# Two transformer blocks on one core: float32r masks, second score products over 128 rows, and ten modulation chunks on VectorE

## The chip, the cores and the metric

The kernel runs on one core of a Trainium2 chip. Its five engines work side by side, each through its own list of instructions in order: TensorE (PE in the profile; its weight loads are shown as PEld), VectorE (DVE), ScalarE (ACT), GpSimd (POOL) and SyncE (SP), which here only issues DMAs. The metric is the device time of one execution in microseconds (us), as the median of several runs. Everything before the launch (splitting and reordering of the weights into the layout that the kernel loads) is outside of it.

## The reference

Two transformer blocks over 512 tokens of width 1024, one after the other, in float32.

```python
def first_block(x, c, ...):
    mod = silu(c) @ ada_w + ada_b
    sh1, sc1, ga1, sh2, sc2, ga2 = split(mod, 6)
    h = rmsnorm(x, pre_mix_g) * (1.0 + sc1) + sh1
    y = hybrid_mixer(h, ...)          # gated conv branch + stick-breaking attention
    x = x + ga1 * rmsnorm(y, post_mix_g)
    h = rmsnorm(x, pre_ffn_g) * (1.0 + sc2) + sh2
    y = swiglu_ffn(h, ...)
    return x + ga2 * rmsnorm(y, post_ffn_g)

def second_block(x, positions, ...):
    h = rms_norm(x, attn_norm_w)
    y_ret = retention_group(...)      # 8 heads of 64, scores with decay, causal
    y_mla = mla_group(...)            # 8 latent heads, softmax, causal
    x = x + concat(y_ret, y_mla) @ w_out
    x = x + conv_ffn(rms_norm(x, ffn_norm_w), ...)
    return rms_norm(x, final_norm_w)
```

In stick-breaking attention a query row t sees the keys s < t (strictly), with a = sigmoid(z) times the product of sigmoid(-z) of the keys between; in the latent attention it sees s <= t with a softmax. Both are computed for 128 queries at a time against the keys up to them.

## The kernel before

**Splitting.** Each float32 operand of a large product is split into a hi part (a float32r cast, on ScalarE) and a lo part (the rest, `lo_of`, L210, on VectorE or GpSimd). `mm3` (L205 to L207) adds three float32r products: hi x hi, lo x hi and hi x lo. A product has a stationary operand of up to 128 rows and 128 columns and a moving operand of 128 rows and up to 512 columns.

**Weights.** They come in slabs of 128x1024 in the order of `ORDER`. `emit_slab` issues the load from SP into `w_st` (two buffers, tag "st" of the pool `ring`), casts it to `w_hi` on ScalarE (L187) and makes `w_lo` (L210); the hi and lo tiles are four deep each. A slab is 24 products of 512 columns (8 blocks of rows times 3).

**Order.** The program is written in the order of its stages; the framework lays it out on the engines by its own simulated timeline, so instructions of neighbouring steps interleave. Pools open and close as stages pass, and a tile in a new pool waits for the tiles that had its place in SBUF.

**Modulation chunks.** `ada_acc` (L367 ff.) multiplies a chunk of 256 columns of ada_w by silu(c). Two loads `ad` of 512 KB hold the eight blocks of 128 rows; eight products with 32 stationary columns each (L373, two records each, so 16 in the trace), four side by side in the columns of the array, leave a partial sum in four quarters of a PSUM tile, which VectorE copies (L378). A product with ones then sums over partitions: `ada_cols` (L384) makes a shift and scale for 128 columns of h, `ga_row` (L404 to L406) a row of 256 gate values over all partitions. Eight chunks feed the first norm, eight the second (six of them between stick heads, two beside the merge), four rows of `grow1` are made beside the merge (loop over p after the heads: output projection of the attention, gating, `mh`), and four rows of `grow2` in the first feed-forward, at m = 4, 8, 12 and 16 of its 22 steps (`fin_extra`). Beside the merge the chunks are loaded into the pool `mtmp`, in the feed-forward into the ring's "st" tiles.

**Stick heads.** `evac_stat` makes of q, for each of two heads of a pair (b = 0, 1), a stationary tile with hi in one half of the rows and lo in the other; `evac_mov` makes of k a moving tile with hi in both halves, and `ml`, where each half holds the lo of one head. A block of scores is then a product over 128 rows (L685: hi x hi and lo x hi), one over 64 rows (L686: hi x lo) and the mask (L687), a bf16 product of the identity with a tile of 0 and -1e30, 128 columns. There are 8 heads of 4 blocks, with 128, 256, 384 and 512 columns. The pipeline has three steps per head (scores, transposes, product with v), with slabs of q, k and gate between them, and the depthwise conv's taps run on VectorE, ScalarE and GpSimd beside them.

**Retention.** `ret_head` does the same with roles exchanged (L1057, L1058), without a mask product: GpSimd zeroes the upper triangle (L1067). **Latent heads.** `mla_head` uses `mm3` for a block and then the causal mask (L1195) as a bf16 product.

Small tiles that the change touches: `part` (L672, a spare tile in `combine`), `adab1` (L153, ada_b + 1), `cs4` (L946, four copies of cos and sin, filled at L985 and transposed at L1128), `ident` (128 columns of the constants, used by all transposes, L231).

## Time and profile before

| | |
|---|---|
| median of 3 runs | 1425.65 us (1425.45 to 1426.05) |
| the profiled execution's own time | 1426.3 us |
| its span, first to last instruction | 1424.6 us |
| TensorE busy | 1378.3 us, 97% |
| VectorE busy | 731.9 us, 51% |
| ScalarE busy | 582.1 us, 41% |
| GpSimd busy | 325.1 us, 23% |
| mean granted TensorE clock | 0.991 |

A row of a timeline gives start, duration, engine, line, operation, out<-in, the part of the array that a product uses (rows*columns), shape and type, count, and in brackets the idle time ahead of it and what ended it. Successive products overlap, since each is shown until its last result lands: a 512-column product is shown with 0.39 us, but the next one starts after 0.23. For the cost of a product the distance between two starts is read, not the duration.

### The profile page before, as it was taken

The page shows a single profiled execution, that of the slowest core. Times are in us where ns is not written, and L with a number is a line of the kernel's source. Part 1 is how long each engine was busy: PE and PEld are TensorE (multiplying, and loading weights), DVE is VectorE, ACT ScalarE, POOL GpSimd, SP SyncE. Part 2 cuts the span into 40 slices and gives each one's busy share as a digit, 9 for nine tenths or more (in the row PEclk, how much of TensorE's full clock was granted, in tenths as well). Part 3 has the DMA queues.
Part 4 walks back from the last instruction along what each step waited for, and adds up shares of the span by engine and source line. Part 5 has one row for each costly group of instructions (what it writes and reads, how often), then busy time and mean ns, then how long its engine had stood idle before and what let it go on. Part 6 is the DMA issues. An engine that isn't in the chain of part 4 may idle for free. (4 is left out here: it accounts for less than half of the span.)

```text
span 1424.6 us, 17617 instructions
## 1 busy us (share of the span) xinstructions
PE 1378.3 (97%) x6846; PEld 1119.7 (79%) x6846; DVE 731.9 (51%) x1132; ACT 582.1 (41%) x953; POOL 325.1 (23%) x329
## 2 busy tenths in 40 slices
PE   6999999999989999999999899999999999999998
PEld 4786777877878888888887788787888888888886
DVE  3299868254365332232333754688256655554334
ACT  4457655322244222222223525668345333333222
POOL 2189745321150000000002533377220000000000
PEclk9998999999999999999999999999999999999999
DMA  9422133564323344333232322001233323232321
GB/s 332 139 83 81 58 103 108 170 201 146 133 68 118 126 126 132 112 104 104 89 104 79 126 95 89 30 16 60 83 110 104 101 92 104 89 104 89 104 90 73
DMA packets 44324, 152.20 MB, mean 107 GB/s; under 512 B 4881, under 2 KB 7057, under 8 KB 44241
## 3 DMA queue, kind: packets, MB, share of 16 engines
q1 hardware_dynamic: 42720, 145.90, 31.0%
q0 software_dynamic: 1376, 4.97, 0.9%
q8 instruction: 54, 0.88, 0.3%
q14 instruction: 30, 0.24, 0.1%
q10 hardware_dynamic: 144, 0.21, 0.0%
HBM read 146.86 MB, written 4.19 MB: 106 GB/s over the span
## 5 line engine op out<-in xcount | busy, mean ns | idle before, releaser
L187 ACT CAST w_hi<-w_st 128x1024 fp32r<-128x1024 f32 (+2 forms) x217 | 225.3, 1039 | 395.6 <-PE ps_p L206 125.9
L210 DVE TENSOR_TENSOR w_lo<-w_st,w_hi 128x1024 fp32r<-128x1024 f32 (+2 forms) x179 | 222.4, 1244 | 258.5 <-ACT w_hi L187 256.6
L205 PE MATMUL ps_p<-hh,w_hi 128*128 128x512 f32 (+1 forms) x740 | 278.0, 382 | 1.9 <-ACT hh L266 1.2
L206 PE MATMUL ps_p<-hl,w_hi 128*128 128x512 f32 (+1 forms) x740 | 279.1, 378 | 0.4 <-POOL hl L210 0.4
L207 PE MATMUL ps_p<-hh,w_lo 128*128 128x512 f32 (+1 forms) x740 | 277.9, 376 | 1.4 <-DVE w_lo L210 1.4
L242 POOL TENSOR_TENSOR r<-q,mhalf 128x1 f32<-128x1 f32 x36 | 21.4, 595 | 768.4 <-DVE q L238 723.9
L205 PEld LDWEIGHTS ps_p<-hh,w_hi 128*128 128x128 f32 x740 | 139.4, 190 | 30.8 <-ACT hh L266 2.5
L207 PEld LDWEIGHTS ps_p<-hh,w_lo 128*128 128x128 f32 x740 | 140.4, 190 | 27.7 <-DVE w_lo L210 2.5
L206 PEld LDWEIGHTS ps_p<-hl,w_hi 128*128 128x128 f32 x740 | 140.6, 190 | 26.0 <-POOL hl L210 1.6
L205 PE MATMUL ps_c<-hh,w_hi 128*128 128x512 f32 (+1 forms) x354 | 130.4, 368 | 3.1 <-ACT hh L266 2.0
L206 PE MATMUL ps_c<-hl,w_hi 128*128 128x512 f32 (+1 forms) x354 | 130.0, 368 | 1.1 <-POOL hl L210 1.1
L207 PE MATMUL ps_c<-hh,w_lo 128*128 128x512 f32 (+1 forms) x354 | 128.6, 363 | 0.0
L210 POOL TENSOR_TENSOR w_lo<-w_st,w_hi 128x1024 fp32r<-128x1024 f32 (+1 forms) x38 | 93.1, 2455 | 67.0 <-ACT w_hi L187 47.1
L210 DVE TENSOR_TENSOR gl<-gf,gh 128x512 fp32r<-128x512 f32 x44 | 30.4, 690 | 105.6 <-ACT gh L869 105.5
L869 ACT CAST gh<-gf 128x512 fp32r<-128x512 f32 x44 | 27.4, 622 | 135.1 <-PE ps_p L206 124.1
L205 PEld LDWEIGHTS ps_c<-hh,w_hi 128*128 128x128 f32 x354 | 67.3, 190 | 15.9 <-ACT hh L266 2.5
L206 PEld LDWEIGHTS ps_c<-hl,w_hi 128*128 128x128 f32 x354 | 66.9, 189 | 11.7 <-POOL hl L210 1.3
L207 PEld LDWEIGHTS ps_c<-hh,w_lo 128*128 128x128 f32 x354 | 67.1, 189 | 11.0 <-issue 0.8
L207 PE MATMUL ps_p<-w_hi,gl 128*128 128x512 f32 x176 | 68.5, 389 | 0.0
L206 PE MATMUL ps_p<-w_lo,gh 128*128 128x512 f32 x176 | 68.5, 389 | 0.0
L205 PE MATMUL ps_p<-w_hi,gh 128*128 128x512 f32 x176 | 68.5, 389 | 0.0
L510 DVE SCALAR_TENSOR_TENSOR ps_c<-upad,vec,ps_c 128x512 f32<-128x512 f32 x87 | 60.6, 747 | 0.7
(423 smaller groups left out, 2536.0 us busy)
## 6 DMA issues: line engine op xcount, KB each, us to landing
ad<-in_ada SPq DMA_DIRECT2D x48, 512.0 KB, 4.0
w_st<-in_w_fin SPq DMA_DIRECT2D x44, 512.0 KB, 3.7
w_st<-in_w_up SPq DMA_DIRECT2D x44, 512.0 KB, 3.7
w_st<-in_w_win SPq DMA_DIRECT2D x22, 512.0 KB, 3.7
w_st<-in_w_fout SPq DMA_DIRECT2D x22, 512.0 KB, 3.6
w_st<-in_w_down SPq DMA_DIRECT2D x22, 512.0 KB, 3.7
w_st<-in_w_gate SPq DMA_DIRECT2D x16, 512.0 KB, 3.7
w_st<-in_w_wo SPq DMA_DIRECT2D x16, 512.0 KB, 3.7
```

What stands on the lines that cost most here:

```text
L187: nc.scalar.copy(w_hi[:, :n], w_st[:, :n])
L205: nc.tensor.matmul(out=out, lhsT=lh, rhs=rh, start=start, stop=False)
L206: nc.tensor.matmul(out=out, lhsT=lh, rhs=rl, start=False, stop=False)
L207: nc.tensor.matmul(out=out, lhsT=ll, rhs=rh, start=False, stop=stop)
L210: (eng or nc.vector).tensor_tensor(out=out, in0=src, in1=hi.bitcast(F32), op=ALU.subtract)
L242: nc.gpsimd.tensor_tensor(out=r, in0=q, in1=mhalf[:, 0:1], op=ALU.pow)
L510: nc.vector.scalar_tensor_tensor(out=out, in0=src, scalar=w, in1=acc, op0=ALU.mult, op1=ALU.add)
L869: nc.scalar.copy(gh, gf[:, k, :])
```

## The change

Masks: the three bf16 tiles go. The identity is loaded by itself (`eye`) and cast to a float32r tile `identr`, which also serves the transposes. `mask_tile` loads one 128x128 mask by SP ahead of the stick heads, and one ahead of the latent heads, and casts it on VectorE; the mask product is float32r. Second score products: `ml` becomes a list of two tiles, one for each head of a pair, with zeros in the other half of the rows (`zero_padded`, eight GpSimd copies in all, two sets of two tiles for the stick heads and two for retention), and the product runs over all 128 rows. Modulation: from the merge on `ADA.vector` is set, and `ada_acc` makes the chunk by one scaling and seven multiply-adds of 128x256 on VectorE. Beside this, `part`, `adab1` and the bf16 mask tiles go, `cs4` moves into the latent pool (and its copies with it), and a few tiles take other places (`early_gate`, `split_o`). What was cut from the diff are renamed tags and the smaller constants.

```diff
+        if ADA.vector:
+            acc = ap_.tile([128, 256], F32, tag="acc", name="acc", bufs=ADA.nacc)
+            for hf, ad in enumerate(ads):
+                for b in range(4):
+                    cc = cact[:, 4 * hf + b, 0:1]
+                    if hf == 0 and b == 0:
+                        nc.vector.tensor_scalar(out=acc, in0=ad[:, b, :], scalar1=cc, scalar2=None, op0=ALU.mult)
+                    else:
+                        nc.vector.scalar_tensor_tensor(
+                            out=acc, in0=ad[:, b, :], scalar=cc, in1=acc, op0=ALU.mult, op1=ALU.add
+                        )
+            return acc, pt()[:, 256:512]
...
-    masks = adp.tile([128, 256], F32, tag="masks", name="masks", bufs=1)
-    nc.gpsimd.dma_start(out=masks, in_=a["masks"])
+    eye = adp.tile([128, 128], F32, tag="eye", name="eye", bufs=1)
+    nc.gpsimd.dma_start(out=eye, in_=a["eye"])
     nc.gpsimd.dma_start(out=pos, in_=a["positions"])
+    nc.vector.tensor_copy(identr, eye)
...
-    nc.vector.tensor_scalar(out=adab1, in0=vec[:, _o:_o + 48], scalar1=1.0, scalar2=None, op0=ALU.add)
-    nc.vector.tensor_copy(identb, ident)
-    nc.vector.tensor_copy(strictb, masks[:, 0:128])
-    nc.vector.tensor_copy(causalb, masks[:, 128:256])
+    for _i in (_o + 8, _o + 32):
+        nc.vector.tensor_scalar(
+            out=vec[:, _i:_i + 8], in0=vec[:, _i:_i + 8], scalar1=1.0, scalar2=None, op0=ALU.add
+        )
...
+    def mask_tile(p, j):
+
+        m = p.tile([128, 128], F32R, tag="mask", name="mask", bufs=1)
+        raw = p.tile([128, 128], F32, tag="sp0", name="raw")
+        nc.sync.dma_start(out=raw, in_=a["masks"][:, 128 * j:128 * j + 128])
+        nc.vector.tensor_copy(m, raw)
+        return m
...
+    def zero_padded(p, name):
+
+        t = [[p.tile([128, S], F32R, tag=f"{name}{i}{b}", name=f"{name}{i}{b}", bufs=1) for b in range(2)] for i in range(2)]
+        for i in range(2):
+            for b in range(2):
+                o = halves_of(b)[1]
+                nc.gpsimd.tensor_copy(t[i][b][o], zero[o].broadcast_to([64, S]))
+        return t
+
+    def evac_mov(ps, p, ml):
         t = []
-        ml = p.tile([128, S], F32R, tag="ml", name="ml")
         for b in range(2):
             mt = p.tile([128, S], F32R, tag=f"mv{b}", name=f"mv{b}")
             o, z = halves_of(b)
             nc.scalar.copy(mt[o], ps[o])
             nc.scalar.copy(mt[z], ps[o])
-            lo_of(ml[o], ps[o], mt[o])
+            lo_of(ml[b][o], ps[o], mt[o])
...
-    def combine(ps, h, dst, p):
+    def combine(ps, h, dst):
         o, z = halves_of(h % 2)
-        part = p.tile([128, S], F32, tag="part", name="part", bufs=1)
-        nc.scalar.copy(part[o], ps[z])
-        nc.vector.tensor_tensor(out=dst[o], in0=ps[o], in1=part[o], op=ALU.add)
+        nc.scalar.copy(dst[o], ps[z])
+        nc.vector.tensor_tensor(out=dst[o], in0=ps[o], in1=dst[o], op=ALU.add)
...
-            nc.tensor.matmul(out=z[:, :n], lhsT=qs[b][o, qb], rhs=kl[o, :n], start=False, stop=False)
-            nc.tensor.matmul(out=z[:, qb], lhsT=identb, rhs=strictb, start=False, stop=True)
+            nc.tensor.matmul(out=z[:, :n], lhsT=qs[b][:, qb], rhs=kl[b][:, :n], start=False, stop=False)
+            nc.tensor.matmul(out=z[:, qb], lhsT=identr, rhs=strict, start=False, stop=True)
...
-            qk[p] += evac_mov(ps, qkp)
+            qk[p] += evac_mov(ps, qkp, kz[p % 2])
...
+    strict = mask_tile(apool, 0)
+    kz = zero_padded(qkp, "kz")
...
-    ADA.pool, ADA.tag, ADA.bufs = mtmp, "ad", 2
+    ADA.pool, ADA.tag, ADA.bufs, ADA.vector = mtmp, "ad", 2, True
...
+    rstk, qz = {}, zero_padded(rt, "qz")
...
+        rstk[p] = (ks,) + evac_mov(ps, rt, qz[p % 2])
...
-            nc.tensor.matmul(out=z[:, :n], lhsT=ks[b][o, js], rhs=ql[o, kb * 128:], start=False, stop=True)
+            nc.tensor.matmul(out=z[:, :n], lhsT=ks[b][:, js], rhs=ql[b][:, kb * 128:], start=False, stop=True)
...
+        cs4 = mla.tile([128, NT, 4, 32], F32)
+        for j in range(4):
+            nc.gpsimd.tensor_copy(cs4[:, :, j, :], sinp if j % 2 else cosp)
...
-            nc.tensor.matmul(out=z[:, qb], lhsT=identb, rhs=causalb, start=False, stop=True)
+            nc.tensor.matmul(out=z[:, qb], lhsT=identr, rhs=latent["causal"], start=False, stop=True)
...
-    latent["mt"] = mt
+    latent.update(mt=mt, causal=mask_tile(mt, 1))
```

## Rows read from the trace of the kernel before

**Rows 1.** Rows of the page, section 1 (busy time, share of the span and instructions of each engine) and of section 6 (DMA issues: out<-in, engine, operation, count, KB each, median us to landing).

```profile
PE 1378.3 (97%) x6846; PEld 1119.7 (79%) x6846; DVE 731.9 (51%) x1132; ACT 582.1 (41%) x953; POOL 325.1 (23%) x329
...
ad<-in_ada SPq DMA_DIRECT2D x48, 512.0 KB, 4.0
```

**Rows 2.** Rows of TensorE's waits (tile and line that waited, what ended it, us in total, times, longest).

```profile
PE ps_t L373 <- DMA ad<-in_ada: 11.9, 1, 11.9
...
PE ps_p L685 <- ACT mv L616: 2.1, 1, 2.1
```

**Rows 3.** Rows of TensorE's timeline in a plain stretch between stick heads; from the first row to the last there are nineteen products of 512 columns, one start after another.

```profile
150.64 0.39 PE L206 MATMUL ps_p<-hl,w_hi 128*128 128x512 f32 x1
...
154.97 0.39 PE L207 MATMUL ps_p<-hh,w_lo 128*128 128x512 f32 x1
```

**Rows 4.** Rows of TensorE's timeline around a chunk in the first feed-forward.

```profile
592.50 0.39 PE L207 MATMUL ps_p<-hh,w_lo 128*128 128x512 f32 x1
...
592.82 1.07 PE L373 MATMUL ps_t<-ad,cact 128*32 128x256 f32 x16
...
594.16 0.40 PE L206 MATMUL ps_p<-hl,w_hi 128*128 128x512 f32 x1
```

**Rows 5.** Rows of TensorE's timeline around a chunk beside the merge; the four products of 512 columns are the one of the first row, two in the middle (lines left out) and one ahead of the last row.

```profile
300.69 0.40 PE L207 MATMUL ps_p<-oh,w_lo 128*128 128x512 f32 x1
...
301.02 0.64 PE L373 MATMUL ps_t<-ad,cact 128*32 128x256 f32 x8
...
303.18 0.39 PE L205 MATMUL ps_c<-hh,w_hi 128*128 128x512 f32 x1
```

**Rows 6.** Rows of VectorE's groups by line in 290 to 342 us (line, engine, operation, out<-in, shapes, count, busy us, mean ns of one, idle before).

```profile
L378 DVE COPY acc<-ps_t 128x256 f32<-128x256 f32 x6 | 2.5, 421 | 2.8 <-PE ps_t L373 2.7
...
L406 DVE SCALAR_TENSOR_TENSOR grow<-grow,gr 128x256 f32<-128x256 f32 x3 | 1.3, 418 | 0.0
```

**Rows 7.** Rows of TensorE's timeline around an isolated block of a stick head.

```profile
237.09 0.39 PE L685 MATMUL ps_c<-mv,st 128*128 128x512 f32 x1
...
237.41 0.49 PE L686 MATMUL ps_c<-ml,st 64*128 64x512 f32 x1
...
237.83 0.23 PE L687 MATMUL ps_c<-strictb,identb 128*128 128x128 bf16 x1
...
238.18 0.40 PE L207 MATMUL ps_p<-hh,w_lo 128*128 128x512 f32 x1
```

**Rows 8.** Rows of TensorE's timeline at the end of a stick head's product with v (L650), successive rows.

```profile
177.25 0.28 PE L650 MATMUL ps_t<-ah,v 128*128 128x256 f32 x1
177.37 0.23 PE L650 MATMUL ps_t<-al,v 128*128 128x128 f32 x1
177.43 0.27 PE L650 MATMUL ps_t<-ah,v 128*128 128x128 f32 x1
177.54 0.44 PE L685 MATMUL ps_p<-mv,st 128*128 128x512 f32 x1
```

**Rows 9.** Rows of TensorE's timeline in retention: first and second score products in turn.

```profile
908.84 0.44 PE L1057 MATMUL ps_p<-mv,st 128*128 128x384 f32 x1
...
909.57 0.38 PE L1057 MATMUL ps_p<-mv,st 128*128 128x256 f32 x1
...
910.20 0.33 PE L1057 MATMUL ps_c<-mv,st 128*128 128x128 f32 x1
```

**Rows 10.** Rows of the same in retention, later: two second products in one row.

```profile
917.04 0.45 PE L1058 MATMUL ps_p<-ml,st 64*128 64x384 f32 x2
```

**Rows 11.** Rows of TensorE's timeline in the latent heads, successive rows.

```profile
949.65 0.23 PE L1195 MATMUL ps_p<-causalb,identb 128*128 128x128 bf16 x1
949.69 0.47 PE L205 MATMUL ps_p<-kT,qh 128*128 128x512 f32 x1
950.00 0.39 PE L206 MATMUL ps_p<-kT,qh 128*128 128x512 f32 x1
```

**Rows 12.** Rows of the weight loads by line and shape (count, busy us, mean ns of one).

```profile
L205 PEld LDWEIGHTS ps_p<-hh,w_hi 128*128 128x128 f32 x740 | 139.4, 190 | 30.8 <-ACT hh L266 2.5 <-ACT w_hi L187 1.9 <-issue 1.6
...
L1195 PEld LDWEIGHTS <-identb 128*128 128x128 bf16 x32 | 3.1, 96 | 3.6 <-issue 2.9
```

**Rows 13.** Rows of busy time by stretch: from:to and length, then busy us and count of PE, PEld, DVE, ACT, POOL, then granted clock, DMA share and GB/s.

```profile
100.00:160.00 60.00, 56.50 (x233) 43.06 (x233) 58.21 (x81) 42.83 (x77) 55.33 (x40) 0.89 0.21 63
...
290.00:342.00 52.00, 52.00 (x287) 36.30 (x286) 25.05 (x38) 13.31 (x17) 8.63 (x6) 1.00 0.58 196
```

**Rows 14.** Rows of the answer on line L985 (GpSimd's copies into cs4: durations in ns, first and last start), and of the timeline of GpSimd, and of all engines, toward the end of retention.

```profile
L985 POOL COPY cs<-cosp x2: 292/293/294, 799.3 to 799.8; 128x128 f32<-128x128 f32 x2
...
925.61 0.29 POOL L1067 TENSOR_SCALAR_AFFINE_SELECT ah<-ah 128x128 fp32r<-128x128 f32 x1 [11.41 <-DVE va L1090]
...
934.84 0.69 DVE L1181 TENSOR_TENSOR qf<-ps_p,trig 128x512 f32<-128x512 f32 x1
```

**Rows 15.** Rows of the timelines of ScalarE, VectorE and SP around the chunk of rows 4.

```profile
581.82 1.05 ACT L187 CAST w_hi<-w_st 128x1024 fp32r<-128x1024 f32 x1 [3.90 <-PE ps_p L206]
...
597.34 1.05 ACT L187 CAST w_hi<-w_st 128x1024 fp32r<-128x1024 f32 x1 [9.25 <-DMA w_st<-in_w_fin]
...
592.99 0.69 DVE L885 TENSOR_TENSOR gf<-sg,ps_p 128x512 f32<-128x512 f32 x1 [8.86 <-PE ps_p L207]
...
593.52 7.80 SPq L186 DMA_DIRECT2D w_st<-in_w_fin  x4
```

More of the change, by code (lines that the diff above doesn't have):

```diff
@@ L53 @@
 ROWS = ("post_mix_g", "ga1", "post_ffn_g", "ga2", "final_norm_w_2")
-C_ID, C_KDEC, C_QDEC, C_FREQ = 0, 128, 160, 192
-NCONST = 224
+C_KDEC, C_QDEC, C_FREQ = 0, 32, 64
+NCONST = 96
 ORDER = (
@@ L120, in build @@
     edge, _ = pool("edge", side="right")
-    edge.tile([128, 96], F32, name="edge")
+    edge.tile([128, 80], F32, name="edge")
     hpool, _ = pool("hpool", side="right")
@@ L143, in build @@
     cst = const.tile([128, NCONST], F32)
-    identb = const.tile([128, 128], BF16)
-    strictb = const.tile([128, 128], BF16)
-    causalb = const.tile([128, 128], BF16)
     ones = const.tile([128, 128], F32)
@@ L152, in build @@
     cact = const.tile([128, 8, 32], F32)
-    adab1 = const.tile([128, 48], F32)
     modA = const.tile([128, 2, 8], F32)
@@ L163, in build @@
     hl = hpool.tile([128, KB, S], F32R)
-    ident = cst[:, C_ID:C_ID + 128]
+    identr = const.tile([128, 128], F32R)
+    ident = identr.bitcast(F32)
     def vcol(name, i):
@@ L356, in build @@
         pool, tag, bufs, nacc = ring, "st", NST, 1
-        loaded = {}
+        loaded, vector = {}, False
     def ada_load(chunk):
@@ L391, in ada_cols @@
         nc.vector.scalar_tensor_tensor(
-            out=modA[:, i, kb:kb + 1], in0=ps[:, 1:2], scalar=adab1[:, sc:sc + 1], in1=vcol(g_name, kb),
+            out=modA[:, i, kb:kb + 1], in0=ps[:, 1:2], scalar=vcol("ada_b", sc), in1=vcol(g_name, kb),
             op0=ALU.add, op1=ALU.mult,
@@ L607, in evac_stat @@
         return t
-    def evac_mov(ps, p):
+    def zero_padded(p, name):
[6 more added lines that the diff above has]
+    def evac_mov(ps, p, ml):
         t = []
-        ml = p.tile([128, S], F32R, tag="ml", name="ml")
         for b in range(2):
@@ L704, in stick_head @@
             ofs[p] = endp.tile([128, S], F32, tag="of", name="of", bufs=2)
-        combine(av(lambda kb, h: v1[:, kb, h, :], h, at), h, ofs[p], apool)
+        combine(av(lambda kb, h: v1[:, kb, h, :], h, at), h, ofs[p])
         yield
@@ L747, in early_gate @@
     def early_gate(m):
-        st = qkp.tile([128, S], F32R, tag=("st0", "st1", "ml", "mv0")[m], name="st")
+        st = qkp.tile([128, S], F32R, tag=("st0", "st1", "kz00", "mv0")[m], name="st", bufs=1 if m == 2 else 2)
         return st.bitcast(F32)
@@ L777, in split_o @@
         o_hi = endp.tile([128, S], F32R, name=f"oh{p}") if p < 3 else qkp.tile([128, S], F32R, tag="mv1", name="oh3")
-        o_lo = endp.tile([128, S], F32R, name=f"ol{p}") if p < 2 else qkp.tile(
-            [128, S], F32R, tag=("ml", "st0")[p - 2], name=f"ol{p}"
-        )
+        if p < 2:
+            o_lo = endp.tile([128, S], F32R, name=f"ol{p}")
+        else:
+            o_lo = qkp.tile([128, S], F32R, tag=("kz01", "st0")[p - 2], name=f"ol{p}", bufs=p - 1)
         oh.append(o_hi)
@@ L945, in build @@
     lp, lp_s = pool("lp")
-    cs4 = lp.tile([128, NT, 4, 32], F32)
     kp4 = lp.tile([128, NT, 4, 32], F32)
@@ L983, in build @@
     cT = cp.tile([128, NT, 384], F32)
-    for j in range(4):
-        nc.gpsimd.tensor_copy(cs4[:, :, j, :], sinp if j % 2 else cosp)
     epsq = cp.tile([128, 2], F32)
@@ L1021, in build @@
     tok_rope(win2_group(0), rq)
-    rstk = {}
+    rstk, qz = {}, zero_padded(rt, "qz")
     def ret_stack(p):
@@ L1029, in ret_stack @@
         transposes(ps, [rq[:, tt, p * 128:(p + 1) * 128] for tt in range(NT)])
-        rstk[p] = (ks,) + evac_mov(ps, rt)
+        rstk[p] = (ks,) + evac_mov(ps, rt, qz[p % 2])
     gen = win2_group(2)
@@ L1049, in ret_head @@
         p, b = divmod(h, 2)
-        o, _ = halves_of(b)
         ks, qs, ql = rstk[p]
@@ L1072, in ret_head @@
         vt = lambda kb, h: v3[h // 4][:, kb, h % 4, :]
-        combine(av(vt, h, (ah, al)), h, of2[:, p, :], rt)
+        combine(av(vt, h, (ah, al)), h, of2[:, p, :])
         yield
@@ L1342, in _constants @@
     c = np.zeros((128, NCONST), np.float32)
-    c[:, C_ID:C_ID + 128] = np.eye(128)
     lg = np.log1p(-(2.0 ** (-5.0 - np.arange(NH))))
@@ L1360, in layout @@
     d["const"] = _constants()
+    d["eye"] = np.eye(128, dtype=np.float32)
     q, k = np.arange(128)[:, None], np.arange(128)[None, :]
```

1 line of the change is left out of this document (removed).

## Prediction

> **What bounds the kernel now.** I read the page first, then TensorE's waits, then its timeline in each stage that the change touches. TensorE is busy for 97% of the span, and VectorE, ScalarE and GpSimd for 51, 41 and 23% [rows 1]. Its waits are few: one of 11.9 us at the start for the first modulation chunk, one of 2.1 us ahead of the first score, and little more [rows 2]. A busy share counts overlapping instructions, so the useful measure is the distance between the starts of successive products. In a plain stretch nineteen products of 512 columns take from 150.64 to 154.97, 0.228 us from start to start [rows 3]. I call that the floor; 256 columns have 0.12 and 128 columns 0.06 us [rows 8], and 384, halfway between 256 and 512, 0.174. Where the distance is more than the floor and TensorE waits for nothing, the time is lost in TensorE itself. All three places that the change touches are of that kind, so what it takes out there should come off the span nearly one for one, as long as the other engines keep up.
>
> **Modulation chunks, ten of them.** Four are in the first gate of the feed-forward (m = 4, 8, 12, 16), and six run beside the merge (six copies L378 in that window [rows 6]). A chunk is sixteen records of a 128-row, 32-column product. Whole, it takes from 592.50 to 594.16 together with two 512-column products, 1.66 − 2 x 0.228 = 1.20 us [rows 4]. Split in two groups of eight, with four such products, it takes 303.18 − 300.69 − 4 x 0.228 = 1.58 us [rows 5]. For the four in the gate I take 1.20, 4.8 us in all. For the six beside the merge the bounds are 7.2 and 9.5 us; I take 9.0, because the timeline shows most of them split. **Taken off TensorE: 13.8 us.** The product with ones that sums the chunk over partitions stays (L384, L404).
>
> VectorE gets in return, for each chunk, one scaling and seven multiply-adds of 128x256, and loses the copy. A multiply-add of this size from SBUF took 0.418 us (L406), the copy 0.421 [rows 6]. For the scaling I take the copy's time at most and nothing at least. So a chunk adds between 2.5 and 2.9 us, I take 2.8. In 290 to 342 us VectorE is busy for 25.1 of 52 us [rows 13]; six chunks make that 41.9, in a stretch that shall become some 43 us long. It fits on average, since ga_row results are needed only at the boundary after w_o, but hardly. In the gate VectorE stands idle for 8.9 us just ahead of a chunk's copy [rows 15], and 2.8 us go into that. There a gain is possible as well: the two ring buffers that hold a chunk are given back today only when TensorE comes by (the next weight load is issued at 593.52, and the cast waited 9.25 us for it [rows 15]); VectorE can take them when they land. I count that at nothing, since the hi and lo tiles, four deep, cover that wait already.
>
> **Second score products of the stick heads, 32 blocks.** An isolated block (L685, L686, mask L687) with the 512-column product behind it takes from 237.09 to 238.18, 1.09 us [rows 7]. The floors are 3 x 0.228 = 0.68 and the mask. L686 uses 64 rows; TensorE starts it 0.32 us after L685, and what follows it 0.42 us after it. With 128 rows and zeros for the other half it has the shape of its neighbours. The float32r mask is not in this trace; the nearest row is the 128-column products of L650: two of them together add 0.29 − 0.12 = 0.17 us [rows 8], so 0.06 to 0.11 for one. Saved per block: 1.09 − 0.68 − (0.06 to 0.11) = 0.30 to 0.35, 32 times **9.6 to 11.2; I take 10.4 us**.
>
> The rule that bears on this is in the Trainium skill, TensorEngine Tiling (Array Packing), Key Properties: changing the tiling mode drains the engine, while another tile in the same mode does not. The trace agrees in its place, at the entry and the exit of 64 rows, and so does the chunk of 32 columns.
>
> **Retention's second products, 32 blocks without a mask.** Two blocks in succession, 384 columns each, take from 908.84 to 909.57 for one pair, 0.73 against 0.35: 0.38 us lost; the next pair, of 256 columns, 0.63 against 0.24, 0.39 [rows 9]. No bf16 is near, so the loss belongs to the 64 rows. Where second products stand back to back, they enter and leave once for all of them [rows 10]. If all stood alone, 12.2 us; if all stood in fours, 3 us. Most alternate in the timeline, about 25 entries: 25 x 0.38 = **9.5 us**.
>
> **Masks of the latent heads, 32.** Mask and the 512-column product behind it take 0.35 us, so the mask 0.12 [rows 11]; the float32r one 0.06 to 0.11. Saved 0.3 to 1.9, **I take 0.8 us**.
>
> A rule speaks against the masks: TensorE: Matmul & The Clock Gate, Weight-path perf modes, in the Trainium skill says that 128 weights that are not FP32 load by a faster way, which float32r would give up. The rows do show 96 ns for the identity in bf16 and 190 for a float32r load [rows 12]. If all of it showed on TensorE, the result would be 64 x 0.09 = 6 us later; the L650 rows, with loads of that kind, leave at most 0.11 for a mask, so it gets a chance of its own and is left out of the sum.
>
> **What else is added.** Eight zero fills of 64x512 on GpSimd, four ahead of each set of heads: a copy of 128 columns took 0.29 us there [rows 14], so 512 columns some 1.2 us, 4.6 us for four. Retention's hide behind idle GpSimd. Those of the stick heads come where GpSimd is busy for 55.3 of 60 us and VectorE for 58.2 [rows 13]; at worst they hold the first second product by 4.6 us, at best they run earlier, as they read only a constant. I take 0.4. The mask tiles come by SP's queue with a cast on VectorE; a load of eight times the size lands 4.0 us after its issue [rows 1], and if it is issued late, the mask's product and what follows on TensorE wait for it: 0 to 4 us, I take 0.3, because nothing but the tile that lay there before can hold it. The copies of cs4 move behind the last use of rq and rk, 4 x 0.29 us on a GpSimd that then is idle for 11.4 us [rows 14]; the transposes behind them are needed only by the first latent query, at 934.8 us. The identity now needs a DMA and a cast; TensorE waits until 11.9 us for something else [rows 2]. combine copies into its destination instead of a spare tile: same instructions. Each of these is at nothing.
>
> In 100 to 160 us the granted clock is 0.89 and VectorE nearly full [rows 13]. About twelve stick blocks lie there, 3.9 us of saving. I give half back as waits, 2.0, because their scans and conv taps queue on VectorE.
>
> **Sum.** 13.8 + 10.4 + 9.5 + 0.8 = 34.5; less 0.4 + 0.3 + 2.0 = 31.8 us. The profiled execution took 1426.3 us, so 1394.5 by its own count; the median of the three runs is 0.65 us lower, which gives **1394 us**. With every term at its high end and nothing given back the saving is 14.3 + 11.2 + 12.2 + 1.9 = 39.6 us (1386); with every term at its low end, and 4.6 + 4 + 3.9 given back, 12.0 + 9.6 + 3 + 0.3 − 12.5 = 12.4 us (1413).
>
> **Rivals.** (a) VectorE becomes the bound of the merge. For it: 41.9 of 43 us, with w_lo and the merge's own products in the same order. Against: work can slide beyond 342 us. Then the merge keeps its length, 9.0 us lost, and the first stretch gives back all: 1394 + 9 + 2 = 1405. (b) 128 rows drain all the same, so the gain is the chunks' alone: 1394 + 18 = 1412. Against it speaks that full-row products show no such distance. (c) The mask costs what its longer weight load says: 1394 + 6 = 1400. (d) Slower: in the gate, VectorE's multiply-adds queue behind L885, which waits for TensorE for up to 8.9 us [rows 15]; the ring buffers are then held longer, and SP with them. Today the casts of the slabs around a chunk lie 15.5 us apart (581.82, 597.34), and four slabs of 24 products cover 21.8 us, less the cast's 1.05: at most 5.2 us are left. From there on TensorE stops: 8.9 + 2.8 − 5.2 = 6.5 us at each of four chunks, and 2.8 at each of six beside the merge, 43 us in all, 1437. Against: VectorE is idle when a chunk lands. (e) (a) and (b) together, with the start of the stick heads held: 1425.
>
> **How the numbers follow.** Forecast 0.58, (a) 0.21, (b) 0.06, (c) 0.07, (d) 0.05, (e) 0.03. The likeliest gives 1394. The range takes in the forecast's high end, (c), (a) and, toward the low ends of the terms, 4 us beyond (a): 1385 to 1409. About 0.2% is what a measurement of this kernel can tell from no change: faster by more than that 0.92, within it 0.03, slower 0.05.
>
> **What would show it.** Right: the distance from the first to the second score product and on to the mask is a floor each (0.23 us at 512 columns), chunks are gone from TensorE after 290 us, VectorE has some 28 us more there. Wrong: TensorE's waits for VectorE (w_lo, ml, gat) grow by more than 5 us, or a second product still starts 0.3 us or more behind a 512-column first one, or TensorE stops ahead of the first stick or the first latent head.

## The result and the profile after

The changed kernel took 1402.42 us (median of four runs, 1401.74 to 1403.73), the kernel before, on the same chip, 1425.61. The ratio is 0.9838, 95% interval 0.9821 to 0.9855: 23.2 us faster, where 31.8 were forecast. In the profiled executions the span went from 1424.6 to 1400.6 us. The question is thus not whether the change works, but where a quarter of the forecast gain (8.6 of 31.8 us) went.

First the page's busy line of the changed kernel, to be read against [rows 1]:

```profile
PE 1348.2 (96%) x6686; PEld 1119.8 (80%) x6686; DVE 769.5 (55%) x1203; ACT 581.2 (41%) x953; POOL 334.7 (24%) x337
```

TensorE lost 160 records and 30 us of busy time; VectorE gained 71 instructions and 38 us. The span fell by 24 us only: the time in which TensorE stood (span less busy time) grew from 46.3 to 52.4 us. Ten chunks account for the counts: 16 products less each on TensorE; eight instructions for one copy on VectorE. The expected 28 us on VectorE became 38, in part because a multiply-add of a chunk takes longer than L406 in [rows 6] did (0.47 to 0.49 us each in the four chunks of the gate), and in part because six of the chunks' instructions beside the merge took 0.76 to 2.65 us, each while GpSimd ran a pass of its own. Here are the chunks' groups in 285 to 342 us, with 28 of the 42 multiply-adds beside the merge (line, engine, operation, out<-in, shapes, count | busy us, mean ns | idle before):

```profile
L378 DVE SCALAR_TENSOR_TENSOR acc<-ad,cact,acc 128x256 f32<-128x256 f32 x28 | 15.4, 550 | 1.8 <-DMA ad<-in_ada 1.3
...
L376 DVE TENSOR_SCALAR acc<-ad,cact 128x256 f32<-128x256 f32 x5 | 2.1, 425 | 0.0
```

A block of a stick head, on TensorE's timeline (start, us, line, tiles, tile mode, shape):

```profile
209.49 0.33 PE L712 MATMUL ps_c<-mv,st 128*128 128x256 f32 x1
209.66 0.28 PE L713 MATMUL ps_c<-kz,st 128*128 128x256 f32 x1
209.78 0.22 PE L714 MATMUL ps_c<-mask,identr 128*128 128x128 f32 x1
209.84 0.39 PE L712 MATMUL ps_p<-mv,st 128*128 128x384 f32 x1
...
210.30 0.45 PE L712 MATMUL ps_p<-mv,st 128*128 128x512 f32 x1
210.59 0.40 PE L713 MATMUL ps_p<-kz,st 128*128 128x512 f32 x1
210.82 0.22 PE L714 MATMUL ps_p<-mask,identr 128*128 128x128 f32 x1
210.88 0.45 PE L679 MATMUL ps_t<-al,v 128*128 128x512 f32 x1
211.17 0.40 PE L679 MATMUL ps_t<-ah,v 128*128 128x512 f32 x1
```

The second product is now at the floor: 0.23 us from L713 to L714, where L686 to L687 took 0.42 in [rows 7]. The mask starts 0.06 us ahead of what follows, but the 512-column product behind it takes 0.29 instead of 0.23: the mask costs 0.12 us in all. The same stretch as in [rows 7], block and the product behind it, is 211.17 − 210.30 = 0.87 us, against 1.09. The two are not quite alike: the 0.87 us begin behind the mask of another block and have its price in their first product (0.29 us instead of 0.23). Without that it is 0.81 us, 0.28 less than before. Over all 32 blocks, the distances of starts of their products and of the product behind each mask, waits left out, lie above the floors by 14.6 us in the kernel before and by 6.5 us in the changed one: 8.1 us saved, 0.25 a block, from 0.20 at 128 columns to 0.33 at 512. The blocks at a granted clock of 1.00 alone save a little less, 0.18 to 0.26, which would be 7.3 us for 32.

Retention's pairs, to be read against [rows 9]:

```profile
886.95 0.34 PE L1083 MATMUL ps_p<-mv,st 128*128 128x384 f32 x1
887.12 0.35 PE L1084 MATMUL ps_p<-qz,st 128*128 128x384 f32 x1
887.31 0.28 PE L1083 MATMUL ps_p<-mv,st 128*128 128x256 f32 x1
887.42 0.28 PE L1084 MATMUL ps_p<-qz,st 128*128 128x256 f32 x1
887.54 0.22 PE L1083 MATMUL ps_c<-mv,st 128*128 128x128 f32 x1
```

A pair of 384 columns takes 0.36 us (0.73 before), one of 256 columns 0.23 (0.63 before). That is the floor.

So TensorE's products do what was forecast, if not by quite as much. What grew are its waits (tile and line that waited, what ended it, us in total, times, longest). [rows 2] had 11.9 and 2.1; the next in the kernel before were 4.4 us for hl, in four waits, and 2.7 for the score banks of the latent heads, in two. The changed kernel:

```profile
PE ps_t L385 <- DMA ad<-in_ada: 11.9, 1, 11.9
PE ps_t L228 <- DVE xn L252: 3.8, 2, 3.3
PE ps_c L202 <- ACT hh L263: 3.1, 1, 3.1
PE ps_p L712 <- ACT sp L718: 2.9, 2, 2.5
PE ps_t L228 <- DVE hl L259: 2.2, 3, 1.1
PE ps_p L712 <- ACT mv L645: 2.1, 1, 2.1
PE ps_t L228 <- DVE modA L403: 1.9, 2, 1.4
```

Two of them, xn and hh, stand at one place, the boundary after w_o, where the kernel before waits for 0.35 and 1.45 us; L712's 2.5 us stands at 136.84 us in the first stick heads, where the kernel before waited for 1.4.

**The time by stage.** I cut the span where a tile first or last appears on TensorE, and subtracted. The first column runs from the start to the first product that reads oh, the start and the stick heads; "merge" from there to the last product that reads oh; "w_o, gate" to the first that reads gh, which takes in the boundary after w_o and the first feed-forward gate; then to retention's first score, to the first product that reads kT (retention), to the last one (latent heads), and to the end. Each line is one profiled execution, in us; the runs are explained below.

| kernel | start, stick | merge | w_o, gate | next | retention | latent | rest | span |
|---|---|---|---|---|---|---|---|---|
| before | 288.3 | 66.9 | 304.6 | 217.3 | 60.5 | 58.7 | 428.4 | 1424.6 |
| after | 284.7 | 56.6 | 303.2 | 216.5 | 51.5 | 59.6 | 428.5 | 1400.6 |
| e1 chunks alone | 289.3 | 56.6 | 303.6 | 217.3 | 60.7 | 56.4 | 428.5 | 1412.4 |
| e2 chunks back | 285.4 | 66.8 | 304.5 | 216.5 | 51.2 | 60.1 | 428.7 | 1413.2 |
| e3 bf16 masks | 285.1 | 57.0 | 303.5 | 216.5 | 51.2 | 58.7 | 429.3 | 1401.3 |
| e4 gate only | 285.0 | 66.8 | 299.5 | 216.5 | 51.6 | 60.8 | 428.8 | 1409.1 |
| e5 two accumulators | 284.4 | 60.9 | 299.5 | 216.5 | 51.3 | 60.8 | 428.5 | 1401.9 |
| e6 latent mask early | 284.2 | 56.6 | 303.5 | 216.5 | 51.2 | 61.5 | 428.7 | 1402.1 |
| e7 light, after | 280.0 | 56.6 | 303.4 | 216.6 | 51.6 | 60.8 | 428.7 | 1397.7 |
| e8 light, before | 288.1 | 66.8 | 304.2 | 217.2 | 61.0 | 55.6 | 428.5 | 1421.5 |
| e9 light latent | 284.9 | 56.7 | 303.2 | 216.5 | 51.5 | 57.4 | 428.9 | 1399.1 |
| e10 four beside merge | 283.7 | 59.8 | 299.9 | 216.5 | 51.6 | 59.6 | 428.9 | 1400.0 |
| e11 glu chunks too | 279.6 | 56.6 | 303.2 | 216.5 | 51.6 | 59.6 | 428.6 | 1395.7 |
| e12 combined | 283.1 | 59.8 | 299.9 | 216.5 | 51.6 | 60.8 | 428.6 | 1400.3 |

From before to after: stick 3.6, merge 10.3, w_o and gate 1.4, the next stage 0.8, retention 9.0, latent −0.9, rest −0.1, in all 24.1 (24.0 without rounding). The 0.8 is one wait: 148 us into that stage TensorE stands ahead of a transpose, for hl, for 1.16 to 1.20 us in the three kernels that make the copies of cs4 on GpSimd there (before, e1, e8), and for 0.31 to 0.33 us in all the others.

### The profile page after: what moved, and what is told of

It reads as the page before. It is cut to its first block, busy times and chain, and to the rows that moved or that the text cites. A ratio compares the mean times of both kernels' runs of the same rounds, so it can differ in the third digit from the quotient of the medians.

```text
span 1400.6 us, 17393 instructions
## 1 busy us (share of the span) xinstructions
PE 1348.2 (96%) x6686; PEld 1119.8 (80%) x6686; DVE 769.5 (55%) x1203; ACT 581.2 (41%) x953; POOL 334.7 (24%) x337
## 4 chain that ended last, share of the span: by engine, by line
PE 84%; DVE 7%; ACT 3%; issue 2%; POOL 2%; DMA 1%; SPq 0%; POOLq 0%; ACTq 0%; DVEq 0%
PE ps_p L202 17%; PE ps_p L204 16%; PE ps_p L203 16%; PE ps_c L203 8%; PE ps_c L204 8%; PE ps_c L202 7%; PE ps_t L202 2%; PE ps_t L204 2%; PE ps_t L203 2%; PE ps_t L228 2%; DVE kp L719 1%; PE ps_t L679 1%; DVE ps_c L523 1%; PE ps_t L385 1%; DVE w_lo L207 1%
## 5 line engine op out<-in xcount | busy, mean ns | idle before, releaser
L207 DVE TENSOR_TENSOR w_lo<-w_st,w_hi 128x1024 fp32r<-128x1024 f32 (+2 forms) x179 | 222.4, 1244 | 235.5 <-ACT w_hi L184 233.8
L203 PE MATMUL ps_p<-hl,w_hi 128*128 128x512 f32 (+1 forms) x740 | 279.6, 379 | 0.4 <-POOL hl L207 0.4
L207 POOL TENSOR_TENSOR w_lo<-w_st,w_hi 128x1024 fp32r<-128x1024 f32 (+1 forms) x38 | 93.8, 2474 | 57.2 <-ACT w_hi L184 49.0
L207 DVE TENSOR_TENSOR gl<-gf,gh 128x512 fp32r<-128x512 f32 x44 | 30.4, 690 | 105.6 <-ACT gh L899 105.6
L204 PEld LDWEIGHTS ps_c<-hh,w_lo 128*128 128x128 f32 x354 | 67.5, 191 | 10.2
```

The source lines that it names most:

```text
L203: nc.tensor.matmul(out=out, lhsT=lh, rhs=rl, start=False, stop=False)
L204: nc.tensor.matmul(out=out, lhsT=ll, rhs=rh, start=False, stop=stop)
L207: (eng or nc.vector).tensor_tensor(out=out, in0=src, in1=hi.bitcast(F32), op=ALU.subtract)
```

## The experiments

My theory was that TensorE saved what it was priced at and that three places gave part of it back: the boundary after w_o, since the last row chunk ends late on VectorE and w_o's first banks come behind its sum; the first stick heads, which the other engines pace; and the latent heads. The rivals: the products bring less than priced, the float32r masks cost their longer weight load, or the losses are chance. All times are medians of four or more runs, compared with runs of the kernel before on the same chip.

### Parts of the change alone

**e1**, the kernel before with the chunks only:

```diff
-    ADA.pool, ADA.tag, ADA.bufs = mtmp, "ad", 2
+    ADA.pool, ADA.tag, ADA.bufs, ADA.vector = mtmp, "ad", 2, True
```

(with the branch of ada_acc that the change adds.)

> The kernel before with one part of the change: the ten chunks beside the merge and in the first feed-forward gate on VectorE, masks and second products as before. Theory (the last row chunk on VectorE ends late and holds a PSUM bank that w_o wants, which gives back some 3.5 us at the boundary after w_o): 13.8 - 3.5 = 10.3 us less than before, about 1415.3. Rival (the chunks pay in full and the missing 8.4 us are lost elsewhere): 13.8 less, 1411.8.

Measured 1413.35 against 1425.3, ratio 0.9914 (0.9901 to 0.9928): 12.0 us. That lies between theory and rival. The stages say why: the merge is 10.3 us shorter, the w_o and gate stage only 1.0, though four chunks have left it. The same execution had a latent stage 2.3 us shorter, which the chunks don't touch; without it the saving is 9.7, near the theory's 10.3.

**e2**, the changed kernel without the chunks:

```diff
-    ADA.pool, ADA.tag, ADA.bufs, ADA.vector = mtmp, "ad", 2, True
+    ADA.pool, ADA.tag, ADA.bufs = mtmp, "ad", 2
```

> The changed kernel with all ten chunks back on TensorE, masks and second products as changed. Theory: 10.3 us more than the changed kernel, about 1412.7, with the waits for xn and hh after w_o (3.3 and 3.1 us in the changed kernel) gone again. Rival (chunks pay in full): 13.8 more, 1416.2.

Measured 1414.76 against 1425.3, ratio 0.9925 (0.9912 to 0.9939). That is 12.3 us above the changed kernel, between theory and rival, and the waits for xn and hh are 0.3 and 1.5 us again. The products and masks alone bring 10.5 us, where the forecast had 10.4 + 9.5 + 0.8 − 2.7 = 18. So the larger part of the shortfall is here, not in the chunks. Retention has its 9.3; the stick heads have 2.9 of the net 7.7, and the latent heads lost 1.4. The merge took 66.8 us again, and w_o and gate 304.5: without chunks, nothing moves there.

**e4**, only the gate's four chunks on VectorE:

```diff
-    ADA.pool, ADA.tag, ADA.bufs, ADA.vector = mtmp, "ad", 2, True
+    ADA.pool, ADA.tag, ADA.bufs = mtmp, "ad", 2
...
-    ADA.pool, ADA.tag, ADA.bufs = ring, "st", NST
+    ADA.pool, ADA.tag, ADA.bufs, ADA.vector = ring, "st", NST, True
```

> The changed kernel with only the four chunks of the first feed-forward gate on VectorE; the six beside the merge are back on TensorE. Theory (the six save 9.0 to 10.3 us in the merge and give back some 3.5 at the boundary): 5.5 to 6.8 us more than the changed kernel, 1408 to 1409, and the boundary after w_o again without its waits for xn and hh. Rival (nothing is given back there): 9.0 to 10.3 more, 1411.4 to 1412.7.

Measured 1410.38, ratio 0.9893 (0.988 to 0.9907): 8.0 us more than the changed kernel, between the two. By stages it is plain: w_o and gate 299.5 us, 5.0 less than with no chunk at all (e2), so a chunk in the gate is worth 1.25 us; and 3.7 less than in the changed kernel, which has the same four chunks in the gate. Those 3.7 us are what the six beside the merge give back behind w_o. Latent heads 1.2 us longer make the rest of the difference.

### The boundary after w_o

In the changed kernel the last sum of a row chunk and the first products of w_o stand so (rows of TensorE's timeline):

```profile
341.52 0.39 PE L202 MATMUL ps_c<-w_hi,mh 128*128 128x512 f32 x1
...
352.87 0.59 PE L416 MATMUL ps_t<-acc,ones 128*128 128x256 f32 x2
353.12 0.58 PE L202 MATMUL ps_t<-w_hi,mh 128*128 128x512 f32 x1
...
385.31 0.38 PE L228 MATMUL ps_t<-identr,xn 128*128 128x128 f32 x2
...
389.25 0.44 PE L228 MATMUL ps_t<-identr,xn 128*128 128x128 f32 x2 [3.33 <-DVE xn L252]
392.80 0.58 PE L202 MATMUL ps_c<-hh,w_hi 128*128 128x256 f32 x1 [3.11 <-ACT hh L263]
```

w_o begins in the banks ps_c and ps_p at 341.52, but its first token tile has the two ps_t banks, which the chunks' sums use in turn, and in TensorE's order its products stand behind the last sum, at 352.87. In the kernel before they came first, at 355.41, as the last sum stood at 342.01. So the first token tile starts 11.6 us late. Its last product then stands 12.2 us ahead of the last one of w_o, where it is 14.3 us in the kernel before; its norm is late too, and at the end of w_o there are too few products left to cover it. VectorE had ended that chunk at 349.05, and TensorE did not wait ahead of the sum: the last 3.8 of the 11.6 us come from the order alone that the framework gave to TensorE. The granted clock falls with the waits (windows: from:to, length, then busy us and count of PE, PEld, DVE, ACT, POOL, granted clock, DMA share, GB/s):

```profile
380.00:390.00 10.00, 6.37 (x30) 4.83 (x28) 6.90 (x12) 5.76 (x12) 3.88 (x5) 1.00 0.23 60
390.00:400.00 10.00, 6.65 (x28) 5.84 (x29) 8.72 (x12) 6.23 (x12) 5.13 (x6) 0.50 0.54 178
400.00:410.00 10.00, 9.61 (x80) 9.37 (x80) 5.30 (x10) 3.75 (x7) 6.84 (x9) 0.99 0.00 0
```

0.50 is 1.2 GHz; TensorE had stood for most of 385.45 to 392.80. It ran its first gate products at half speed: those of 256 columns start 0.21 us apart up to 400.2, and 0.12 from there on. The kernel before has such a stretch too, but a shorter one. Here are 20 us around and behind the end of w_o, the kernel before first, then the changed one:

```profile
396.00:416.00 20.00, 16.85 (x108) 14.51 (x106) 16.22 (x24) 12.47 (x24) 11.84 (x14) 0.91 0.38 120
```

```profile
385.00:405.00 20.00, 12.63 (x73) 10.89 (x71) 15.31 (x22) 11.21 (x22) 10.19 (x13) 0.74 0.38 118
```

The granted clock was 0.50 for 3.4 us in the first and for 10.2 us in the second. All fourteen executions of the table fall into these two kinds. Where w_o's products in ps_t stand behind the last sum (the changed kernel, e1, e3, e6, e7, e9, e11), TensorE stands for 7.0 to 7.5 of the 16 us behind w_o, with 10.2 us at 0.50. Where they come first (the kernel before, e2, e4, e5, e8, e10, e12), it stands for 2.1 to 3.0 us, with 3.4 us at 0.50, or 6.8 in e2.

**e5** gives the chunks a second accumulator, so that VectorE need not wait for TensorE's sum between chunks:

```diff
-    ADA.pool, ADA.tag, ADA.bufs, ADA.vector = mtmp, "ad", 2, True
+    ADA.pool, ADA.tag, ADA.bufs, ADA.vector, ADA.nacc = mtmp, "ad", 2, True, 2
...
-            ga_row(0, grow1, accp, q, mtmp)
+            ga_row(0, grow1, mtmp, q, mtmp)
```

(ada_cols beside the merge takes mtmp as well.)

> The changed kernel with two accumulators instead of one for the chunks beside the merge, so that a chunk's first multiply needn't wait until TensorE has summed the chunk before it; same instructions. Theory (the last row chunk ends late and holds a PSUM bank of w_o): the chunks end well ahead of w_o, its products start in all eight banks at once, and the 3.5 us at the boundary come back, 1398.9. Rival (the boundary loses because the merge is shorter or the clock falls there, whatever bank is held): unchanged, 1402.4.

Measured 1403.99, ratio 0.9852 (0.9837 to 0.9867): no gain. The mechanism holds; its price doesn't go away. The rows of e5 (timeline, then a window):

```profile
311.46 0.70 PE L416 MATMUL ps_t<-acc,ones 128*128 128x256 f32 x2 [0.45 <-DVE acc L378]
320.31 0.70 PE L416 MATMUL ps_t<-acc,ones 128*128 128x256 f32 x2 [1.31 <-DVE acc L378]
327.48 0.70 PE L416 MATMUL ps_t<-acc,ones 128*128 128x256 f32 x2 [1.21 <-DVE acc L378]
...
345.52 0.39 PE L202 MATMUL ps_t<-w_hi,mh 128*128 128x512 f32 x1
```

```profile
388.00:408.00 20.00, 16.26 (x107) 14.17 (x106) 16.68 (x25) 12.71 (x26) 12.63 (x15) 0.91 0.38 118
```

The last sum stands at 327.48, w_o starts in ps_t at once, its stage takes 299.5 us with nothing given back, and the clock at the boundary is 0.91. But the chunks, packed closer, are now later than the places that TensorE's order has for their sums: it waits 3.0 us for them, and the merge takes 60.9 us instead of 56.6 (the other 1.3 us are not traced). What is saved behind w_o is paid ahead of it.

**e10** puts the last two of the six back on TensorE:

```diff
         for q in ((0,), (1, 2), (3,), ())[p]:
+            ADA.vector = q < 2
             ga_row(0, grow1, accp, q, mtmp)
```

> The changed kernel with the last two of the six chunks beside the merge back on TensorE. Theory (the chunks on VectorE end too late for w_o): TensorE pays 2.4 to 3.2 us for the two, and the boundary gives its 3.5 back, so 0.3 to 1.1 less, about 1401.7. Rival (the boundary doesn't depend on them): 2.4 to 3.2 more, about 1405.

Measured 1402.24, ratio 0.984 (0.9826 to 0.9853): 0.2 us less than the changed kernel. That is within the noise, near the theory's 0.3 to 1.1 less and below the rival's 1405. The stages decide it: the merge pays 3.2 us for the two, and the boundary returns 3.2, with w_o's products in ps_t first again. Four or six chunks beside the merge are thus worth the same.

### The stick heads

**e7 and e8** are the changed kernel and the kernel before with less to do on the other engines:

```diff
         src, w = upad[:, m, j:j + S], vcol("conv_w", 4 * j + m)
+        if 0 < j < TAPS - 1:
+            acc, out, src = acc[:, 0:128], out[:, 0:128], src[:, 0:128]
```

> The changed kernel with the 29 inner taps of the convolution on 128 of 512 columns (the rest of their work is left out), so that VectorE, ScalarE and GpSimd have room beside the stick heads. Theory (the second products and masks cost TensorE 9 us less in the stick heads, of which the other engines' chain takes back 5 to 6): it stands 27 to 29 us below the equally lightened kernel before, instead of 23.2. Rival (the products themselves bring less than priced): still 23 us below it.

> The kernel before with the 29 inner taps of the convolution on 128 of 512 columns (the rest of their work is left out). It is the other half of the pair: theory 27 to 29 us above the lightened changed kernel, rival 23 us above it. By itself it should gain little, 2 to 5 us, since TensorE waited there for 4.5 us only: 1420 to 1423.

Measured 1399.77 (0.982, 0.9806 to 0.9833) and 1423.35 (0.9984, 0.9975 to 0.9993), 23.6 us apart; e8 by itself gains 2.1 us, as expected. By the end of the kernel that is the rival's number, and the theory's 27 to 29 is a miss. By the stage it is the theory's: the stick heads are 8.1 us shorter in the light pair, 3.6 in the full one. The windows of the stretch 112 to 160 us, e8 first, then e7:

```profile
112.00:160.00 48.00, 44.27 (x187) 33.29 (x186) 19.41 (x28) 25.86 (x52) 26.34 (x23) 0.89 0.20 56
```

```profile
112.00:160.00 48.00, 43.09 (x206) 35.69 (x204) 19.76 (x29) 27.40 (x55) 26.46 (x23) 0.93 0.21 67
```

With VectorE at 20 of 48 us, TensorE gets through 206 records in that time instead of 187. The same window of the kernel before and of the changed kernel themselves:

```profile
112.00:160.00 48.00, 44.50 (x181) 33.13 (x180) 46.57 (x63) 34.76 (x65) 43.49 (x34) 0.86 0.20 56
```

```profile
112.00:160.00 48.00, 41.54 (x184) 33.56 (x183) 46.50 (x61) 34.77 (x65) 41.41 (x33) 0.89 0.19 56
```

VectorE is full in both. TensorE starts 184 records instead of 181, and the 3.0 us that it is busy less stand there as waits. From the first block's first product to the twentieth's it is 59.8 us before and 59.0 after; in the light pair it is 58.9 and 55.1. Over the stage, from the first score on, TensorE stands for 2.4 us before and for 6.4 after.

The light pair's 8.1 us are not products alone. In the stick heads e8 had a granted clock of 0.50 for 13.7 us and e7 for 6.9, while e7 stands for 2.5 us there and e8 for 0.8. But the distances of starts, as above, give 13.7 and 5.7 us over the floors for its 32 blocks, which is 8 us again. The rival is thus half right: the products bring less than priced, 7 to 8 us and not 10.4, and the waits take over half of it back. The 4.5 us more of the light pair were then lost in the latent heads: 55.6 us in e8, 60.8 in e7, the shortest and one of the longest of all.

### The latent heads

**e3**, masks and their identity in bf16 again, 128-row products kept:

```diff
-            nc.tensor.matmul(out=z[:, qb], lhsT=identr, rhs=strict, start=False, stop=True)
+            nc.tensor.matmul(out=z[:, qb], lhsT=identb, rhs=strict, start=False, stop=True)
```

(the mask tile bf16, an identity in bf16, and the latent mask likewise.)

> The changed kernel with both masks and their identity in bf16 again, all second products over 128 rows as changed. Theory (the mask costs the same in either type, 0.12 us with the product behind it): within 1 us of the changed kernel, 1402.4. Rival (the float32r mask pays for its longer weight load, 64 x 0.09 us): 6 us less, 1396.6. Second rival (a bf16 product between float32r ones costs 0.05 us more): 3 us more, 1405.6.

Measured 1403.0, ratio 0.9845 (0.9831 to 0.9858): the mask costs the same in either type. The traces say so too: by the distances of starts, a mask of the latent heads costs 0.12 us with the product behind it in the kernel before, 0.12 in the changed one and 0.11 in e3, in the mean. The gain of 0.8 us from it did not exist, nor did rival (c).

**e6** loads and casts the latent mask during retention:

```diff
+        lm = mla.tile([128, S], F32R, tag="cs4", name="lm", bufs=1)
+        raw = mla.tile([128, S], F32, tag="qf", name="raw", bufs=1)
+        nc.sync.dma_start(out=raw[:, 0:128], in_=a["masks"][:, 128:256])
+        nc.vector.tensor_copy(lm[:, 0:128], raw[:, 0:128])
```

> The changed kernel with the latent heads' mask loaded and cast during retention, into a tile that has lost its use by then, instead of right ahead of the latent heads. Theory (the wait of 0.7 us for the mask and those just behind it are the price of the late load): 0.7 to 2.0 us less, about 1401. Rival (the latent heads are paced by ScalarE, which gives back the score banks): unchanged within 0.5, 1402.4.

Measured 1403.83, ratio 0.9849 (0.9835 to 0.9862): no gain, as the rival said. The wait for the mask is gone, and others grew; the latent stage took 61.5 us.

**e9** shortens VectorE's row maxima there:

```diff
-                nc.vector.tensor_reduce(out=nm, in_=z[:, :n], axis=AX.X, op=ALU.max, negate=True)
+                nc.vector.tensor_reduce(out=nm, in_=z[:, 0:32], axis=AX.X, op=ALU.max, negate=True)
```

> The changed kernel with the row maxima of the latent heads over 32 columns instead of up to 512 and their scores scaled by 0.05 (so the softmax is another one; same instructions). VectorE is busy for 54.7 of 60 us there and loses some 10. Theory (the latent heads are paced by VectorE and ScalarE, which return the score banks late, so what TensorE saves there isn't seen): the waits for those banks (3 to 5 us) mostly go, 2 to 4 us less, 1398.4 to 1400.4. Rival (TensorE paces them and the waits are chance): unchanged within 0.7, 1402.4.

Measured 1400.77, ratio 0.9826 (0.9813 to 0.984): 1.7 us less, short of the 2 to 4 expected; the intervals of e9 and the changed kernel overlap. The windows of the latent heads, the changed kernel first, then e9:

```profile
912.00:972.00 60.00, 55.86 (x366) 48.55 (x365) 54.72 (x126) 46.71 (x112) 43.97 (x45) 1.00 0.14 46
```

```profile
912.00:972.00 60.00, 57.21 (x382) 49.91 (x381) 45.61 (x130) 47.38 (x115) 45.98 (x49) 1.00 0.15 46
```

VectorE had 9 us less to do, and TensorE has 16 records more in the same time. This does not show that VectorE paces the stage: in the changed kernel TensorE is busy for 55.9 of the 60 us and VectorE for 54.7, and the order of the instructions alone does as much. In e4, e5, e7 and e12 every engine has the same instructions in the same order there, and the stage took 60.8 us in each, on three chips. The changed kernel and e11 share another order, and it took 59.6 us in both. e9 has an order of its own.

### Further along the same way

**e11** puts seven of the eight chunks of the first stage on VectorE as well:

```diff
     def glu_in(kb, halves=1):
+        ADA.vector = kb > 0
         ada_cols(0, kb, "pre_mix_g", adp)
```

> The changed kernel with seven more chunks on VectorE: all of the first stage but its first. VectorE is busy there for 13.3 of 40 us. Theory (a chunk costs TensorE 1.24 us wherever it stands, and VectorE is free there): 8.7 us less, 1393.7. Rival (its result comes later from VectorE, some 4 us a chunk, and TensorE waits for the modulation instead): unchanged or up to 5 us more, 1402 to 1407.

Measured 1399.45 (1397.47 to 1402.71), ratio 0.982 (0.9806 to 0.9833): 3.0 us less, neither 8.7 nor nothing; the interval touches the changed kernel's. In the profiled run the first score comes at 109.27 instead of 115.72 us, 6.5 earlier, and a wait of TensorE for a score bank has grown, from 2.5 us in the changed kernel to 4.4:

```profile
PE ps_p L713 <- ACT sp L719: 4.4, 1, 4.4
```

In that execution the first product that reads oh comes only 5.1 us earlier, so the stick heads took 1.3 us back at once.

**e12** takes e11 and e10 together, and the last two chunks beside the stick heads on VectorE too:

```diff
+                ADA.vector = kb > 3
                 ada_cols(1, kb, "pre_ffn_g", accp)
```

> The changed kernel with seven chunks of the first stage and the last two beside the stick heads on VectorE as well, and the last two beside the merge back on TensorE: thirteen chunks from TensorE to VectorE where it has room, two the other way. Theory (a chunk is worth 1.0 to 1.2 us where VectorE has room, and the stretch of the first stick heads takes back more than half of what comes before it): 3.0 and 0.2 us less by the two runs before, and 2.0 for the two chunks in a stretch where VectorE is busy for half the time, 1397.2. Rival (the two beside the stick heads hold the transposes' PSUM banks and pay nothing): 1399.2.

Measured 1401.51 (1399.43 to 1402.07), ratio 0.9822 (0.9808 to 0.9835): about the changed kernel's time. Both expectations were too low. In its execution the stick stage gained only 1.6 us on the changed kernel, and TensorE waits 2.3 us for al (L207) ahead of transposes, 1.9 of it at once. That fits the rival's mechanism, but one execution doesn't show it. Of all kernels that compute the same, e11 has the lowest median, by an amount that these runs do not separate from the changed kernel.

## Why the prediction came out as it did

The direction, the mechanism on TensorE and the range held; the sum was 8 us too large. Step by step:

- **Chunks in the gate**: forecast 4.8, measured 5.0 to 5.1 (e4 against e2). Right. Rival (d), slower because VectorE holds the ring, did not happen (its four slabs are 21.9 us and not 21.8, which changes nothing).
- **Chunks beside the merge**: forecast 9.0, with bounds of 7.2 and 9.5. The merge became 10.3 us shorter, in e1 as in the changed kernel: all six chunks stood split in two, and one cost 1.7 us instead of 1.58. What failed is the step "it fits on average, since ga_row results are needed only at the boundary after w_o": w_o's first banks come behind the sum of the last one, and 3.7 us come back behind w_o. I had used "work can slide beyond 342 us" as the argument against rival (a). It slid, and this was its price. Neither rival (a) nor the forecast had the place right; e5 shows that the loss can be moved into the merge but does not go away.
- **Second products of the stick heads**: forecast 10.4, measured 7 to 8. Two things were mis-sized: the mask costs 0.12 us with the slower product behind it, not 0.06 to 0.11, and the isolated block of [rows 7] stood for all 32. A block of 512 columns saves 0.25 to 0.33 us, near the forecast, one of 128 columns 0.18 to 0.20.
- **Give-back in the first stick heads**: forecast 2.0 + 0.4 + 0.3 = 2.7. Measured 8.1 − 3.6 = 4.5: the first score comes 0.5 us later, and TensorE stands for 4.0 us more behind it. "I give half back" was a guess at the middle of 0 and 3.9; with VectorE at 46.5 of 48 us hardly anything from that stretch came off the span. e11 says the same from the other side: time saved ahead of it is partly taken back in it.
- **Waits**: "and little more" was a misreading of the kernel before. TensorE stood for 46.3 us there, and the two waits that the prediction names are 14.0 of them. So the sum had no line for what the others would become.
- **Retention**: forecast 9.5, measured 8.8 to 9.3 in every kernel with the change. The count was right: the trace has 25 visits to 64 rows. The price was not. By the distances of starts the score products lose 7.8 us less, 0.31 a visit instead of 0.38. About 1 us more came from the clock, for which there was no term: in this stage it was granted at 0.50 for 6.8 us before and for 3.4 after. That the total came so near is in part luck.
- **Latent masks**: forecast 0.8 saved; the stage became 0.9 us longer. The mask costs the same in both types (e3), so the rule of the Trainium skill that spoke against it (TensorE: Matmul & The Clock Gate, Weight-path perf modes: 128 weights that are not FP32 load faster) decides nothing here. The larger error was to take the length of the stage for TensorE's products: it was 55.6 to 61.5 us over all runs, and two orders of the same heads took 59.6 and 60.8. So the 0.9 cannot be put down to the masks.
- **Ahead of retention**: the 0.8 us there were in no term. They go with the copies of cs4, which the prediction moved at no price and no gain; no run moves these copies alone.
- Rival (b) was wrong: 128 rows start without the loss in and out of 64. The other costs that I put at nothing cost nothing that shows.

With these sizes: 10.3 + 5.1 − 3.7 + 3.6 + 9.0 − 0.9 + 0.8 = 24.2, against 24.0 in the profiled spans.

What stays open: what paces the latent heads, and why they took 55.6 to 58.7 us in the kernels with the old masks and second products, and 57.4 to 61.5 in the others. e3, with bf16 masks, had 58.7, e9 57.4 with its lighter maxima. Each is one execution, and their orders of instructions differ; where the order is the same, the time is too. e6 shows that it is not the mask's load.

## What to carry to other kernels

Price a product by the distance of starts where it stands, with the product behind it, and for each size that occurs; one isolated case multiplied by 32 was over a quarter too much. Ask of every engine that takes over work not only whether it has room on average, but which shared buffer the work holds until it is done, and who wants that buffer next: here the late sum of one chunk, with two PSUM banks behind it, cost a third of what the six chunks had saved. Where a stretch has another engine at 97%, count what TensorE saves there at nothing rather than at half: here twenty blocks brought 0.8 us. And before a stage's length is put down to a change, compare the order of its instructions: here another order of the same heads made 1.2 us.

## What I had not expected of the hardware

A float32r product of 128 columns starts the next product after 0.06 us, but that next one of 512 columns then takes 0.29 us to its successor instead of 0.23; a bf16 one of the same size costs the same 0.12 us in all. A multiply-add of 128x256 on VectorE from SBUF took 0.47 to 0.49 us with the chunk as operand, not 0.42. Of the lines and shapes that VectorE runs four times or more, 27 instructions of the kernel before and 36 of the changed one took over 0.3 us longer than the median of their kind; every one of them overlaps a GpSimd instruction, and together they lost 23 and 34 us. Most VectorE instructions beside a long GpSimd pass were not slowed, and the runs do not show what makes the difference. And with a stop of TensorE of some 7 us, a few products in between (385.45 to 392.80), the granted clock was 0.50 for 10.2 us from 390.0 on; in the kernel before and in e5, whose longest wait there is 1.45 us, it was 0.50 for 3.4 us.
